# Moving the first G slice and the second X slice of a weight-gradient matmul from hardware to software DMA queues

## The chip, the cores and the metric

One core of one Trainium2 chip. The metric is the device time of the whole program in microseconds (us), as the median of several runs on one chip. The profile comes from one of those runs and counts its own span, some 1.7 us less than the device time.

The kernel before takes 176.0 us (three runs, 175.95 to 176.5).

## The reference

```python
# input 16 x 512 x 1024, grad_output 16 x 512 x 768, both float32
grad_weight = np.einsum('bmk,bmn->kn', input, grad_output)   # 1024 x 768
```

Batch and m are one contraction of 8192 rows. The kernel cuts it into 64 slices of 128 rows: X[s] is 128 x 1024, G[s] is 128 x 768. Each slice costs 12 matmuls of 512 columns, eight "wide" ones (the first 512 columns of G) and four "narrow" ones (the other 256, with G as the weights).

## The kernel before

Data is float32 in memory and bfloat16 in the matmuls. There are two ways to get it there. The loads on the *software queue* (issued by GpSimd) write bfloat16 tiles from the float32 data (its packets are counted at 1536 bytes for a row of 768). Those on the *hardware queues* (issued by sync and scalar) write float32 tiles here, which casts on the vector engine (DVE, 0.29 us for 128 x 256) or ScalarE (ACT, 0.41 us) then convert. Slice 0 and X of slice 1 come by hardware, all else by software. While data is under way, PE multiplies constants as a warm-up (0.78 to 5.42 us). Its matmuls of 512 columns start 0.427 us apart; the real ones, from the second at 5.69 us on, 0.2155 us. Below these are called half rate and full rate.

```python
ORDER = (          # A, B: wide halves; N: narrow; number: up to which slice; "!": close the sums
    "A1! B1 N1 B2! N2 A2 N3! A3 B3 A4! B5 N5 B6! N7 A6 N8! A9! B10 N9 B12! N12! A12! "
    ...
WARMUP = [512] * 10 + [128] * 2
...
    xf = [head.tile([P, K], f32, name=f"xf{s}") for s in range(2)]
    gf = head.tile([P, N], f32, name="gf")
    nc.sync.dma_start(out=gf[:, 0:NA], in_=G[0:P, 0:NA])
    nc.scalar.dma_start(out=xf[0], in_=X[0:P, :])
    nc.sync.dma_start(out=gf[:, NA:N], in_=G[0:P, NA:N])
    nc.scalar.dma_start(out=xf[1], in_=X[P : 2 * P, :])
    ...                                             # warm-up matmuls on constants
    for s in range(1, S):
        gt = xg.tile([P, N], bf16, name="gt")
        nc.gpsimd.dma_start(out=gt, in_=G[s * P : (s + 1) * P, :])
        ...
        if s > 1:
            xs[s] = xg.tile([P, K], bf16, name="xt")
            nc.gpsimd.dma_start(out=xs[s], in_=X[s * P : (s + 1) * P, :])
    ...                                             # twelve casts of g0, x0, x1
    for k in range(KS):                             # the last 14 slices, group by group
        slices = range(parts["A" if k < KS // 2 else "B"].done, S)
        pieces = [(0, NA)] if k < KS - 1 else [(0, 256), (256, 384), (384, NA)]
        for c0, c1 in pieces:
            ...                                     # matmuls of one bank
            add_out(acc[:, k, c0:c1], bank)
            W = NB if k < 6 else c1 - c0
            for c in range(c0, c1, W):
                nc.sync.dma_start(out=OUT[:, k, c : c + W], in_=acc[:, k, c : c + W])
```

Of the kernel before, what the change touches and what calls it, by code (L numbers as in the profile page):

```python
# [8 lines left out]
P = 128  # L9
NA = 512  # L10
# [6 lines left out]
ORDER = (  # L17
    "A1! B1 N1 B2! N2 A2 N3! A3 B3 A4! B5 N5 B6! N7 A6 N8! A9! B10 N9 B12! N12! A12! "
    "B15 AB17! n17! AB26! n26! AB41! n41! AB47 A50! B50! N64!"
).split()  # L20

WARMUP = [512] * 10 + [128] * 2
XBUFS = 42


# [1 line left out]
def kernel(  # L27
# [6 lines left out]
    nc = tc.nc  # L34
    bf16 = mybir.dt.bfloat16
    f32 = mybir.dt.float32

    B, M, K = input.shape
    _, _, N = grad_output.shape
    S = B * M // P  # L40
    KS = K // P
    NB = N - NA
# [3 lines left out]
    X = input.rearrange("b m k -> (b m) k")  # L46
    G = grad_output.rearrange("b m n -> (b m) n")
    OUT = out.rearrange("(ks p) n -> p ks n", p=P)

    head = ctx.enter_context(tc.tile_pool(name="head", bufs=1))  # L50
# [11 lines left out]
    xs = [None] * S  # L62
    gwide = [None] * S
    gnarrow = [None] * S
# [2 lines left out]
    ctx.enter_context(tc.manual_schedule(engines={E.PE, E.DVE, E.Activation}))  # L67


    xf = [head.tile([P, K], f32, name=f"xf{s}") for s in range(2)]  # L70
    gf = head.tile([P, N], f32, name="gf")
    nc.sync.dma_start(out=gf[:, 0:NA], in_=G[0:P, 0:NA])
    nc.scalar.dma_start(out=xf[0], in_=X[0:P, :])
    nc.sync.dma_start(out=gf[:, NA:N], in_=G[0:P, NA:N])
    nc.scalar.dma_start(out=xf[1], in_=X[P : 2 * P, :])


    ones = nc.const_aps.tensor(1.0, (P, P), bf16)
    wps = psum.tile([P, NA], f32, name="bank7")
    for i, cols in enumerate(WARMUP):  # L80
        nc.tensor.matmul(  # L81
# [5 lines left out]
        )  # L87


    for s in range(1, S):  # L90
        gt = xg.tile([P, N], bf16, name="gt")
        nc.gpsimd.dma_start(out=gt, in_=G[s * P : (s + 1) * P, :])  # L92
        gwide[s] = gt[:, 0:NA]
        gnarrow[s] = gt[:, NA:N]
        if s > 1:
            xs[s] = xg.tile([P, K], bf16, name="xt")
            nc.gpsimd.dma_start(out=xs[s], in_=X[s * P : (s + 1) * P, :])  # L97

    for s in range(2):
        xs[s] = head.tile([P, K], bf16, name=f"x{s}")  # L100
    g0 = head.tile([P, N], bf16, name="g0")
    gwide[0] = g0[:, 0:NA]
    gnarrow[0] = g0[:, NA:N]

    def round_by(engine, dst, src, c0, c1):
        copy = nc.vector.tensor_copy if engine == "DVE" else nc.scalar.copy
        copy(out=dst[:, c0:c1], in_=src[:, c0:c1])  # L107

    round_by("DVE", g0, gf, 0, 256)
    round_by("ACT", g0, gf, 256, NA)  # L110
    round_by("DVE", xs[0], xf[0], 0, P)
    round_by("ACT", xs[0], xf[0], 2 * P, 4 * P)
    round_by("DVE", xs[0], xf[0], P, 2 * P)
    round_by("DVE", xs[0], xf[0], 4 * P, 6 * P)
    round_by("ACT", xs[0], xf[0], 6 * P, 8 * P)

    def add_out(dst, src):
        nc.vector.tensor_add(out=dst, in0=src, in1=dst)  # L118

    def copy_out(dst, src, i):  # L120
        if i % 2 == 0:
            nc.vector.tensor_copy(out=dst, in_=src)  # L122
        else:
            nc.scalar.copy(out=dst, in_=src)  # L124

    def wide_mm(bank, k, s, start, stop, c0=0, c1=NA):
        nc.tensor.matmul(  # L127
            bank, xs[s][:, k * P : (k + 1) * P], gwide[s][:, c0:c1], start=start, stop=stop
        )
# [34 lines left out]
    def add_slice(part, i, s, first, last):  # L164
        group = part.groups[i]
        name, bank = part.banks[i]
        part.matmul(bank, *group, s, first, last)
        if not last:
            return
        dst = part.dst(*group)  # L170
        if part.first:
            copy_out(dst, bank, i)
            if s == 0 and i == 0:
                round_by("DVE", g0, gf, NA, N)
        else:
            add_out(dst, bank)
        if part is parts["N"] and s == S - 1:
            t, h = group
            hb = NA // SQ
            nc.vector.transpose(  # L180
                out=turned[:, h * hb : (h + 1) * hb, :, t],
                in_=dst.rearrange("p (b r) -> p b r", r=SQ),
            )
        free.append(name)
        del part.banks[i]
        if not part.banks:
            part.first = False

    def slice_by_slice(names, upto, close):
        while any(parts[n].done < upto for n in names):  # L190
            for n in names:
                part = parts[n]
                s = part.done
                if s == upto:
                    continue
                part.done += 1
                first = not part.banks
                for i in range(len(part.groups)):
                    if first:
                        open_bank(part, i)  # L200
                for i in range(len(part.groups)):
                    add_slice(part, i, s, first, close and s == upto - 1)

    def bank_by_bank(part, upto):
        first = part.done
        part.done = upto
        for i in range(len(part.groups)):
            open_bank(part, i)
            for s in range(first, upto):
                add_slice(part, i, s, s == first, s == upto - 1)  # L210

    for i, step in enumerate(ORDER):
        if i == 2:

            round_by("DVE", xs[1], xf[1], 4 * P, 6 * P)
            round_by("ACT", xs[1], xf[1], 6 * P, 8 * P)
            round_by("DVE", xs[1], xf[1], 0, 2 * P)
            round_by("ACT", xs[1], xf[1], 2 * P, 4 * P)
        close = step.endswith("!")
        names = step.rstrip("!").rstrip("0123456789")  # L220
        upto = int(step.rstrip("!").lstrip("ABNn"))
        if names.islower():
            bank_by_bank(parts[names.upper()], upto)
        else:
            slice_by_slice(names, upto, close)

    rows_of = out.rearrange("(b r) n -> r b n", r=SQ)
    for a in range(P // SQ):
        c = NA + a * NT * SQ
        nc.scalar.dma_start(  # L230
            out=rows_of[:, :, c : c + NT * SQ],
            in_=turned[a * SQ : (a + 1) * SQ].rearrange("p b r t -> p b (r t)"),
# [2 lines left out]

    for k in range(KS):
        slices = range(parts["A" if k < KS // 2 else "B"].done, S)
        pieces = [(0, NA)] if k < KS - 1 else [(0, 256), (256, 384), (384, NA)]
        for c0, c1 in pieces:
            name = free.pop(0)  # L240
            bank = psum.tile([P, NA], f32, name=name)[:, 0 : c1 - c0]
            for s in slices:
                wide_mm(bank, k, s, s == slices[0], s == slices[-1], c0, c1)
            add_out(acc[:, k, c0:c1], bank)
            free.append(name)
            W = NB if k < 6 else c1 - c0
            for c in range(c0, c1, W):
                nc.sync.dma_start(out=OUT[:, k, c : c + W], in_=acc[:, k, c : c + W])

# [29 lines left out]
```

## Time and profile before

| | before |
|---|---|
| device time, median | 176.0 us |
| span in the profile | 174.3 us |
| matrix engine (PE) busy | 169.9 us, 97% |
| 768 real matmuls at 0.2155 us | 165.5 us |
| first real matmul starts | 5.32 us |
| last add starts | 171.50 us |

Read it from both ends: since PE is the chain throughout, a change that leaves the matmuls alone can move only the start, the end, or open holes between. The prediction below shows the page, the chain, both ends and the queues.

```profile
28.78 1.03 PE L134 MATMUL bank<-xt,gt 128*128 128x512 bf16 x4
29.64 1.89 PE L127 MATMUL bank<-gt,xt 128*128 128x512 bf16 x8
31.37 1.89 PE L134 MATMUL bank<-xt,gt 128*128 128x512 bf16 x8
```

In the lines of a timeline below (start, length, engine, operation, count) gt and xt are bfloat16 tiles of G and X, gf and xf float32 ones, and out<-in stands before the sizes. The eight wide matmuls at 29.64 are slices 10 and 11 ("B12!" in the order, four each). Slice 11 is used from the fifth on, at 29.64 + 4 x 0.2155 = 30.50 us. Its X landed at 30.16 by the trace. So there is no wait, but there is only about 0.3 us to spare.

### The profile page before, as it was taken

How to read it: one execution, taken by the hardware profiler on the slowest of the kernel's cores; microseconds unless marked ns; L12 is line 12 of the kernel's file. 1: busy time of each engine (PE TensorE's matmuls, PEld its weight loads, DVE VectorE, ACT ScalarE, POOL GpSimd, SP SyncE). 2: the span in 40 equal slices, each digit the busy share in tenths (PEclk: the TensorE clock that was granted, in tenths of full speed). 3: DMA queues.
4: the chain of work that ended last, by engine and by line, in shares of the span. 5: the costliest groups of instructions: out<-in, count | busy, mean ns of one | idle time of the engine just before them, and what ended most of it. 6: DMA issues, size and time to landing. Idle time of an engine off the chain costs nothing.

```text
span 174.3 us, 2013 instructions
## 1 busy us (share of the span) xinstructions
PE 169.9 (97%) x793; PEld 78.4 (45%) x808; DVE 61.3 (35%) x103; ACT 6.2 (4%) x12; POOL 66.7 (38%) x129
## 2 busy tenths in 40 slices
PE   8999999999999999999999999999999999999993
PEld 3444444444444444444444444444444444444463
DVE  0655582883940039300000662200560003931122
ACT  2640000000000000000000000000000000000000
POOL 7444434444444444444444444444274200000000
PEclk9999999999999999999999999999999999999999
DMA  5999999999999999999999999999999990085623
GB/s 192 276 208 209 207 209 208 208 208 209 207 208 209 207 208 210 207 209 209 206 209 208 208 210 207 207 209 208 207 209 209 207 202 11 0 190 160 170 86 120
DMA packets 25048, 33.35 MB, mean 191 GB/s; under 512 B 6480, under 2 KB 16592, under 8 KB 25040
## 3 DMA queue, kind: packets, MB, share of 16 engines
q0 software_dynamic: 18000, 28.65, 89.9%
q10 hardware_dynamic: 4448, 2.10, 4.7%
q1 hardware_dynamic: 2592, 2.49, 4.2%
q8 instruction: 6, 0.10, 0.2%
q14 instruction: 2, 0.02, 0.0%
HBM read 58.72 MB, written 3.15 MB: 355 GB/s over the span
## 4 chain that ended last, share of the span: by engine, by line
PE 97%; issue 0%; DVE 0%
PE bank L127 63%; PE bank L134 32%; PE bank L81 3%; DVE acc L118 0%
## 5 line engine op out<-in xcount | busy, mean ns | idle before, releaser
L127 PE MATMUL bank<-gt,xt 128*128 128x512 bf16 (+2 forms) x515 | 108.3, 367 | 0.5
L127 PEld LDWEIGHTS <-xt 128*128 128x128 bf16 x524 | 50.2, 98 | 57.2
L118 DVE TENSOR_TENSOR acc<-bank,acc 128x512 f32<-128x512 f32 (+2 forms) x62 | 37.9, 667 | 73.4 <-PE bank L127 72.9
L134 PE MATMUL bank<-xt,gt 128*128 128x512 bf16 x242 | 54.8, 379 | 0.3
L97 POOL DMA_DIRECT2D xt<-in_input_dram x62 | 33.1, 533 | 38.7 <-DMA xt<-in_input_dram 36.5
L92 POOL DMA_DIRECT2D gt<-in_grad_output_dram x63 | 33.8, 536 | 31.2 <-DMA gt<-in_grad_output_dram 24.9
L134 PEld LDWEIGHTS <-gt 128*128 128x128 bf16 x252 | 24.6, 98 | 29.7
L118 DVE TENSOR_TENSOR acct<-bank,acct 128x512 f32<-128x512 f32 x24 | 15.7, 682 | 30.0 <-PE bank L134 29.9
L81 PE MATMUL bank<-const-bfloat16-1.0 128*128 128x512 bf16 (+1 forms) x12 | 4.6, 574 | 0.8 <-PEq L263 0.8
L81 PEld LDWEIGHTS <-const-bfloat16-1.0 128*128 128x128 bf16 x12 | 1.6, 140 | 3.5 <-issue 3.5
L122 DVE COPY acc<-bank 128x512 f32<-128x512 f32 x4 | 2.7, 687 | 1.0 <-PE bank L127 1.0
L180 DVE STREAM_TRANSPOSE turned<-acct 128x512 f32<-128x512 f32 x4 | 2.9, 715 | 0.1
L127 PEld LDWEIGHTS <-x 128*128 128x128 bf16 x16 | 1.6, 98 | 1.9 <-DVE x L107 0.2
L107 DVE CAST g<-gf 128x256 bf16<-128x256 f32 x2 | 0.6, 290 | 4.7 <-DMA gf<-in_grad_output_dram 4.7
L124 ACT COPY acc<-bank 128x512 f32<-128x512 f32 x4 | 2.1, 589 | 1.3 <-PE bank L127 1.3
L127 PE MATMUL bank<-gt,x 128*128 128x512 bf16 x8 | 2.1, 379 | 0.0
L127 PE MATMUL bank<-g,x 128*128 128x512 bf16 x8 | 2.0, 398 | 0.0
L122 DVE COPY acct<-bank 128x512 f32<-128x512 f32 x2 | 1.3, 686 | 1.3 <-PE bank L134 1.3
L107 ACT CAST x<-xf 128x256 bf16<-128x256 f32 x4 | 1.4, 409 | 0.0
L107 ACT ACT_TABLE_LOAD x1 | 1.3, 1283 | 1.7 <-PEq L263 1.7
L124 ACT COPY acct<-bank 128x512 f32<-128x512 f32 x2 | 1.1, 588 | 1.5 <-PE bank L134 1.5
L107 DVE CAST x<-xf 128x256 bf16<-128x256 f32 (+1 forms) x5 | 1.0, 260 | 0.0
(8 smaller groups left out, 3.3 us busy)
## 6 DMA issues: line engine op xcount, KB each, us to landing
xt<-in_input_dram POOLq DMA_DIRECT2D x62, 256.0 KB, 8.5
gt<-in_grad_output_dram POOLq DMA_DIRECT2D x63, 192.0 KB, 8.5
out_dram<-acc SPq DMA_DIRECT2D x13, 128.0 KB, 2.7
xf<-in_input_dram ACTq DMA_DIRECT2D x2, 512.0 KB, 5.1
out_dram<-turned ACTq DMA_DIRECT2D x4, 256.0 KB, 3.4
gf<-in_grad_output_dram SPq DMA_DIRECT2D x1, 256.0 KB, 3.9
out_dram<-acc SPq DMA_DIRECT2D x1, 256.0 KB, 2.0
gf<-in_grad_output_dram SPq DMA_DIRECT2D x1, 128.0 KB, 4.7
```

What stands on the lines that cost most here:

```text
L81: nc.tensor.matmul(wps[:, 0:cols], ones, nc.const_aps.tensor(1.0, (P, cols), bf16), start=True, stop=True,)
L92: nc.gpsimd.dma_start(out=gt, in_=G[s * P : (s + 1) * P, :])
L97: nc.gpsimd.dma_start(out=xs[s], in_=X[s * P : (s + 1) * P, :])
L107: copy(out=dst[:, c0:c1], in_=src[:, c0:c1])
L118: nc.vector.tensor_add(out=dst, in0=src, in1=dst)
L122: nc.vector.tensor_copy(out=dst, in_=src)
L124: nc.scalar.copy(out=dst, in_=src)
L127: nc.tensor.matmul(bank, xs[s][:, k * P : (k + 1) * P], gwide[s][:, c0:c1], start=start, stop=stop)
L134: nc.tensor.matmul(bank, gnarrow[s].rearrange("p (r t) -> p t r", t=NT)[:, t], xs[s][:, h * NA : (h + 1) * NA], start=start, stop=stop,)
L180: nc.vector.transpose(out=turned[:, h * hb : (h + 1) * hb, :, t], in_=dst.rearrange("p (b r) -> p b r", r=SQ),)
```

## The change

Its intent: have only X of slice 0 go through the hardware queues and the casts, half of its rows on each queue; let the software queue, whose tiles need no cast, bring all of G and the other X. The warm-up is cut a little, and the last output bank is finished in two pieces in place of three.

```diff
-WARMUP = [512] * 10 + [128] * 2
+WARMUP = [512] * 9 + [128] * 4
...
-    xf = [head.tile([P, K], f32, name=f"xf{s}") for s in range(2)]
-    gf = head.tile([P, N], f32, name="gf")
-    nc.sync.dma_start(out=gf[:, 0:NA], in_=G[0:P, 0:NA])
-    nc.scalar.dma_start(out=xf[0], in_=X[0:P, :])
-    nc.sync.dma_start(out=gf[:, NA:N], in_=G[0:P, NA:N])
-    nc.scalar.dma_start(out=xf[1], in_=X[P : 2 * P, :])
+    xf = head.tile([P, K], f32, name="xf")
+    nc.sync.dma_start(out=xf[0 : P // 2], in_=X[0 : P // 2, :])
+    nc.scalar.dma_start(out=xf[P // 2 : P], in_=X[P // 2 : P, :])
...
-    for s in range(1, S):
+    for s in range(S):
...
-        if s > 1:
+        if s > 0:
...
+    xs[0] = head.tile([P, K], bf16, name="x0")   # in place of twelve casts
+    for c in range(0, K, 512):
+        nc.vector.tensor_copy(out=xs[0][:, c : c + 256], in_=xf[:, c : c + 256])
+        nc.scalar.copy(out=xs[0][:, c + 256 : c + 512], in_=xf[:, c + 256 : c + 512])
...
-        pieces = [(0, NA)] if k < KS - 1 else [(0, 256), (256, 384), (384, NA)]
+        pieces = [(0, NA)] if k < KS - 1 else [(0, 384), (384, NA)]
...
-            W = NB if k < 6 else c1 - c0
+            W = P if k == 0 else NB if k < KS - 1 else c1 - c0
```

More of the change, by code (lines that the diff above doesn't have):

```diff
@@ L94 @@
         gnarrow[s] = gt[:, NA:N]
-        if s > 1:
+        if s > 0:
             xs[s] = xg.tile([P, K], bf16, name="xt")
             nc.gpsimd.dma_start(out=xs[s], in_=X[s * P : (s + 1) * P, :])
-    for s in range(2):
-        xs[s] = head.tile([P, K], bf16, name=f"x{s}")
-    g0 = head.tile([P, N], bf16, name="g0")
-    gwide[0] = g0[:, 0:NA]
-    gnarrow[0] = g0[:, NA:N]
-    def round_by(engine, dst, src, c0, c1):
-        copy = nc.vector.tensor_copy if engine == "DVE" else nc.scalar.copy
-        copy(out=dst[:, c0:c1], in_=src[:, c0:c1])
-    round_by("DVE", g0, gf, 0, 256)
-    round_by("ACT", g0, gf, 256, NA)
-    round_by("DVE", xs[0], xf[0], 0, P)
-    round_by("ACT", xs[0], xf[0], 2 * P, 4 * P)
-    round_by("DVE", xs[0], xf[0], P, 2 * P)
-    round_by("DVE", xs[0], xf[0], 4 * P, 6 * P)
-    round_by("ACT", xs[0], xf[0], 6 * P, 8 * P)
+    xs[0] = head.tile([P, K], bf16, name="x0")
+    for c in range(0, K, 512):
+        nc.vector.tensor_copy(out=xs[0][:, c : c + 256], in_=xf[:, c : c + 256])
+        nc.scalar.copy(out=xs[0][:, c + 256 : c + 512], in_=xf[:, c + 256 : c + 512])
     def add_out(dst, src):
@@ L172, in add_slice @@
             copy_out(dst, bank, i)
-            if s == 0 and i == 0:
-                round_by("DVE", g0, gf, NA, N)
         else:
@@ L210, in bank_by_bank @@
                 add_slice(part, i, s, s == first, s == upto - 1)
-    for i, step in enumerate(ORDER):
-        if i == 2:
-            round_by("DVE", xs[1], xf[1], 4 * P, 6 * P)
-            round_by("ACT", xs[1], xf[1], 6 * P, 8 * P)
-            round_by("DVE", xs[1], xf[1], 0, 2 * P)
-            round_by("ACT", xs[1], xf[1], 2 * P, 4 * P)
+    for step in ORDER:
         close = step.endswith("!")
```

## The prediction

> **What bounds the kernel now.** I began with the page: how busy each engine is, and the chain that ended last.
>
> ```profile
> span 174.3 us, 2013 instructions
> PE 169.9 (97%) x793; PEld 78.4 (45%) x808; DVE 61.3 (35%) x103; ACT 6.2 (4%) x12; POOL 66.7 (38%) x129
> ...
> PE 97%; issue 0%; DVE 0%
> PE bank L127 63%; PE bank L134 32%; PE bank L81 3%; DVE acc L118 0%
> ```
>
> The matrix engine is the chain from one end to the other. 3% of it is warm-up on constants (L81), the rest real matmuls. The work asks for 64 slices x (8 wide + 4 narrow) = 768 matmuls of 512 columns. In the chain of waits four of them take 0.86 us, so 0.2155 us each and 768 x 0.2155 = 165.5 us. The diff changes none of these, so it can act only on the head (before the first real matmul), on the tail (after the last), or by opening a hole in between. I therefore read the timeline at both ends. The head:
>
> ```profile
> 0.74 0.41 ACTq L73 DMA_DIRECT2D xf<-in_input_dram  x1
> 0.74 0.38 SPq L72 DMA_DIRECT2D gf<-in_grad_output_dram  x1
> ...
> 0.78 4.64 PE L81 MATMUL bank<-const-bfloat16-1.0 128*128 128x512 bf16 x12 [0.78 <-PEq L263]
> ...
> 1.23 1.20 POOL L92 DMA_DIRECT2D gt<-in_grad_output_dram  x2 [0.79 <-POOLq L263]
> ...
> 4.71 0.29 DVE L107 CAST g<-gf 128x256 bf16<-128x256 f32 x1 [4.71 <-DMA gf<-in_grad_output_dram]
> ...
> 5.04 0.56 DVE L107 CAST x<-xf 128x128 bf16<-128x128 f32 x3
> ...
> 5.32 2.04 PE L127 MATMUL bank<-g,x 128*128 128x512 bf16 x8
> ...
> 7.78 0.53 POOL L97 DMA_DIRECT2D xt<-in_input_dram  x1 [2.05 <-DMA gt<-in_grad_output_dram]
> ```
>
> Real work starts at 5.32 us, when the casts of slice 0 are ready, and the warm-up was sized to end there (0.78 + 4.64 = 5.42). From 5.32 to the last add at 171.50 is 166.2 us, 0.7 us over the matmuls' own 165.5; so there is no hole to close. The last line shows that the first G slice on the software queue had landed by 7.78 us: GpSimd, its eight completion semaphores used up, waited for it. The tail:
>
> ```profile
> 169.94 0.42 DVE L118 TENSOR_TENSOR acc<-bank,acc 128x256 f32<-128x256 f32 x1 [0.84 <-PE bank L127]
> 170.72 0.29 DVE L118 TENSOR_TENSOR acc<-bank,acc 128x128 f32<-128x128 f32 x1 [0.36 <-PE bank L127]
> 171.50 0.29 DVE L118 TENSOR_TENSOR acc<-bank,acc 128x128 f32<-128x128 f32 x1 [0.49 <-PE bank L127]
> ```
>
> After 171.50 come 0.29 us of add, the last 64 KB store (issue to landing 1.5 us) and the program's end: 174.3 - 171.5 = 2.8 us.
>
> Then the view that decides this case, the DMA queues from 1 to 5.25 us. Software descriptors were being issued from 1.23 us on, yet the software queue (q0) has no line there:
>
> ```profile
> q10 hardware_dynamic: 214, 0.81, 50.7%
> q1 hardware_dynamic: 286, 0.39, 28.8%
> ```
>
> From 5.25 to 6.5 us it has 89 packets. So its first byte moved some 4 us after its first issue, just as the smaller hardware queue (q1) ran empty. Whether that is its own start-up time or starvation by the two hardware queues, this trace can't say, and the new kernel puts the very first G on that queue.
>
> [...] warm-up weight loads come 0.42 to 0.43 us apart, twice the 0.2155 of later.
>
> **The change, part by part.**
>
> *Removed:* hardware loads of G slice 0 (384 KB) and X slice 1 (512 KB), and seven of the eleven casts. The vector engine (35% busy) and ScalarE (4%) are off the chain after 5.3 us; the casts are worth nothing by themselves.
>
> *X of slice 0:* 512 KB, half on each hardware queue. By the half-microsecond view DMA moved at 111, 201 and 250 GB/s from 1.5 to 3.0 us, which is 281 KB, then at about 410. So 524 kB are moved by 3.0 + 243/410 = 3.6 us. Landing lags: wide G and first X, 786 kB, by the same sum were moved at 4.2 and released their readers at 4.71 and 5.04, up to 0.8 later. X lands at about 4.4. The cast is now four pieces, two per engine; the first pair ends after 0.29 (DVE) and 0.41 (ACT), so the first half of X is ready at 4.8 and the rest at 5.2. X alone would let the matmuls start near 5.0.
>
> *G of slice 0* on the software queue decides. Its copy reads 393 kB; GpSimd's waits end 0.97 us apart for one G slice (7.78, 8.75) and 1.23 for one X slice, so the queue moves one G in 0.97 us. (a) If it shares from the start[...], X and G together, 917 kB, are moved at 3.0 + 636/410 = 4.55 and land at about 5.35. (b) If it starves while the hardware queues are full, it begins at about 3.6 plus a gap that I guess at 0.5, moves 0.97, lags 0.8: 5.85. (c) If 4 us from issue is its own start-up, it begins at 5.28, moves 0.97, lags 0.6 to 0.8: about 7.0.
>
> *Warm-up:* 9 x 0.427 + 4 x 0.107 = 4.27 us against 10 x 0.427 + 2 x 0.107 = 4.48, so it ends 0.21 us sooner. This gains only if data is there by 5.1. That someone sized it so finely speaks for (a).
>
> *Slices 1 and on:* X of slice 0, G0, G1, X1 are the same 1.835 MB that had landed by 7.78 before, so X1 lands at about 7.8 to 8.0 in (a) and (b). It is needed 12 matmuls (2.6 us) after the start, at 8.0 or later: no hole. After that loading takes 0.97 + 1.23 = 2.20 us a slice against 12 x 0.2155 = 2.59 of matmuls, so it stays ahead. The window of the loads from slice 42 on is unchanged.
>
> *Tail:* 384 + 128 columns in place of 256 + 128 + 128. By the difference of the adds' starts a 128-column round of 14 slices takes 0.78 us and a 256-column one 1.53, so three pieces cost 3.09 and two 3.02 + about 0.03: 0.03 us saved. The 384 store (192 KB) is issued about half a microsecond ahead of the last 64 KB and could delay it by up to 0.1. The rest of the output pieces (first group in four, seventh in two) lie 3 us or more before the end; 24 hardware DMAs in both. Tail: 0 to +0.1.
>
> *Sum.* Starts of 5.4 (a), 5.9 (b), 7.05 (c) against 5.32: +0.1, +0.6, +1.7. Against this the first real matmul took 0.37 us to the next one in the timeline, 0.15 over the warm rate; a later start pays less of that: -0.1 in (a) and (b). [...] With +0.05 for the tail: (a) +0.05, (b) +0.5, (c) +1.8 to 2.3. I give (a) half, (b) three tenths, (c) a fifth, and predict 176.2 us, just above (a).
>
> **The rivals.** *Slow software start (c):* for it, the empty q0 until 5.25; against it, the coincidence with q1 running empty, and the tuned warm-up. It would make 177.8 to 178.3. *A real gain:* if the software queue shares at once and landing is quick, the start is bounded by 917 kB at the measured rate, so not before 5.15, and then at half clock: 175.8 at best. *A hole at slice 1*, in place of the wait removed: X1 has only 0.0 to 0.3 us to spare and would leave a hole of some tenths[...]; 176.4. *Tail queueing* behind the 192 KB store: 176.1 to 176.2 alone.
>
> **Range and chances.** The run-to-run spread before is 0.3% (175.95 to 176.5). 175.6 leaves room for the best gain; 177.8 takes in the lower end of (c). Faster by 2% would be 172.5, sooner than the head can give even if real work began at 1.8 us: as good as excluded. Slower by 2% needs 179.5, G0 landing after 8.8: 2 in 100.
>
> **What would show it.** Right: the first L111 matmul between 5.3 and 5.9, released by the landing of gt rather than by a cast; q0 packets before 4.5 us; 166 us from there to the last add; 2.8 us after. Wrong: q0 silent until 5.2 again (then (c)); a wait of the matrix engine for xt at about 8; more than 2.9 us from the last add on; or the granted clock dropping after the warm-up.

The sum came to +0.05 us in (a), +0.5 in (b) and +1.8 to 2.3 in (c), on 176.0. One term of it is cut: in (c), up to +0.5 for half-rate matmuls after 2 us of idleness. So the 1.8 is 1.7 + 0.05 rounded, and the 2.3, like the rival's 178.3, has the term in it; the predicted 176.2 was set just above (a), where it plays no part. Case (a), the queues sharing from the start, was the author's assumption: in the trace of the kernel before the software queue had no packet until 5.28 us. The gap of 0.5 us in (b) and the 0.1 us for the 192 KB store are guesses. Measured later: the software queue's first packet 0.01 us after the last hardware load's first completion (3.93 and 3.92), and 0.03 us more from the last add to the end. The eight semaphores are in the trace: GpSimd issued eight loads by 5.11 us, each on a semaphore of its own, and the ninth only at 7.78, after the first had landed at 7.49.

## The result, and the profile after

The changed kernel took 176.86 us (median of four runs, 176.59 to 177.08), against 176.03 (175.95 to 176.5) of the kernel before in the same rounds. Executions over 1.5% slower than the fastest of the same kernel are left out of the means. A ratio here is the mean time of one kernel's fast runs over that of the other's fast runs of the same rounds, so not quite the ratio of the medians quoted: 1.0041, with a 95% interval of 1.0018 to 1.0063. That is within 2%, and slower by some tenths of a microsecond.

The page of the kernel after: span, busy time, and the chain that ended last.

```profile
span 175.1 us, 1997 instructions
PE 170.7 (97%) x795; PEld 77.5 (44%) x795; DVE 60.2 (34%) x97; ACT 5.2 (3%) x9; POOL 67.4 (38%) x131
...
PE bank L111 53%; PE bank L118 27%; DMA xt<-in_input_dram 15%; POOL gt L89 1%; POOL xt L94 1%; DVE acc L102 0%; POOLq L239 0%
```

PE was the whole chain before. Now 15% of it is the landing of xt, and the chain in order of time (start, length, what) shows where that ends:

```profile
21.99 9.28 DMA xt<-in_input_dram
31.27 0.05 issue
31.31 1.04 PE bank L111 x4
```

Up to 31.27 us the latest event is a transfer; only from there on is it matmuls alone. So some X slice reached PE late at 31 us. The share of 15% is no measure of loss: that loading ran beside matmuls, and what was lost is only the waits of PE. They are in the timeline, first at the head (in brackets: idle before, and what ended it).

```profile
0.73 0.55 SPq L71 DMA_DIRECT2D xf<-in_input_dram  x1
0.74 0.56 ACTq L72 DMA_DIRECT2D xf<-in_input_dram  x1
...
4.31 1.28 ACT L99 ACT_TABLE_LOAD   x1 [4.31 <-DMA xf<-in_input_dram]
5.31 0.59 DVE L98 CAST x<-xf 128x256 bf16<-128x256 f32 x2 [5.31 <-DMA xf<-in_input_dram]
...
5.80 1.89 PE L111 MATMUL bank<-gt,x 128*128 128x512 bf16 x8 [0.60 <-DMA gt<-in_grad_output_dram]
7.52 1.03 PE L118 MATMUL bank<-x,gt 128*128 128x512 bf16 x4
...
8.52 1.04 PE L111 MATMUL bank<-gt,xt 128*128 128x512 bf16 x4
```

Real work starts at 5.80, 0.48 later than before, and what released it is the landing of G's first slice at 5.76. The first cast of X was done only at 5.71, so X by itself would have held the start almost as long. The first 12 matmuls then run at full rate: eight in 7.52 - 5.80 = 1.72 us, 0.215 each. In the kernel before 12 took 5.32 to 8.06, 2.74 against 2.59 at full rate, so 0.15 us of half-rate work is no longer paid. But at 7.52 + 4 x 0.2155 = 8.38 slice 1 is due, its X landed at 8.48, and the matmul starts at 8.52: a hole of 0.14. The second hole is at slice 11:

```profile
30.12 1.03 PE L111 MATMUL bank<-gt,xt 128*128 128x512 bf16 x4
31.31 1.04 PE L111 MATMUL bank<-gt,xt 128*128 128x512 bf16 x4 [0.17 <-DMA xt<-in_input_dram]
```

Slice 11 was due at 30.12 + 4 x 0.2155 = 30.98 and came at 31.31, a hole of 0.33. (The bracket shows 0.17, because matmul ends are modelled: each such record is 0.38 us long where the next starts after 0.2155. The starts are the better measure.) X11 landed at 31.27 here and at 30.16 before: 1.1 later, while the matmuls had become only 0.48 later, and the 0.3 to spare was not enough. In the trace each load raises its semaphore 16 times, read here as one for its part on each of the 16 DMA engines, and PE went on after the last of them. Here a single one was late: the other 15 were in by 30.53, in time for 30.98, the last at 31.27. From X9 on the last engine lands 0.7 to 0.8 us after the next to last, up to X8 about 0.1; in between a 16 KB packet of the instruction queue (q8) took 0.89 us from 24.65. The kernel before has the same packet at 24.01 and the same jump at X9 (0.1 to 0.9 us). The trace doesn't name the engine, so this link is one of time; if it holds, the hole came from the late head and this packet together.

The tail, as the adds that close the last two groups:

```profile
169.23 0.69 DVE L102 TENSOR_TENSOR acc<-bank,acc 128x512 f32<-128x512 f32 x1 [2.33 <-PE bank L111]
171.50 0.56 DVE L102 TENSOR_TENSOR acc<-bank,acc 128x384 f32<-128x384 f32 x1 [1.58 <-PE bank L111]
172.28 0.29 DVE L102 TENSOR_TENSOR acc<-bank,acc 128x128 f32<-128x128 f32 x1 [0.22 <-PE bank L111]
```

From the seventh group's add to the last add it takes 3.05 us, against 3.09 before (168.41 to 171.50), and from the last add to the end 2.80 against 2.77.

| where | before | after | change, us |
|---|---|---|---|
| first real matmul | 5.32 | 5.80 | +0.48 |
| half-rate loss in the first 12 | 0.15 | 0 | -0.15 |
| hole at slice 1 | 0 | 0.14 | +0.14 |
| hole at slice 11 | 0 | 0.33 | +0.33 |
| last two groups' adds apart | 3.09 | 3.05 | -0.04 |
| last add to end | 2.77 | 2.80 | +0.03 |
| sum | | | +0.79 |

The span grew by 0.8 and the median by 0.83, so the account closes.

**Why is everything loaded a microsecond later?** The same 1.835 MB (X0, G0, G1, X1) had landed at 7.49 before and at 8.48 now, and X2, X3 and X11 are 1.0 to 1.1 late too. The DMA queues from 1 to 5.25 us (packets, MB, share of 16 engines' time), to be held against the same view in the prediction:

```profile
q0 software_dynamic: 154, 0.22, 32.3%
q10 hardware_dynamic: 80, 0.26, 25.2%
q1 hardware_dynamic: 80, 0.26, 22.9%
```

The software queue now runs before 5.25. Its packets are counted as bfloat16 (1536 bytes for a row of 768), so they stand for twice as much float32 (the page counts 58.72 MB read from memory, which is both inputs whole in float32, and 29.11 MB on this queue): the three together moved 0.26 + 0.26 + 2 x 0.22 = 0.96 MB of float32 where two queues had moved 1.20. At the software queue's steady 208 GB/s (206 to 211 in most slices of the page), 416 of float32, the missing 0.24 MB are 0.6 us of the delay by estimate. From 2 to 3 us only one hardware queue has a line:

```profile
q1 hardware_dynamic: 58, 0.23, 88.7%
```

The row halves went one after the other: q1's first packet at 2.07 and its first completion at 3.00 (the trace has 16 packets of 4 bytes at the end of each load, read here as one from each engine and called completions; the semaphore's 16 rises came later, here from 3.79 to 4.24, and the last of them is the landing); q10's first packet at 3.00, its first completion at 3.92; the software queue's first packet at 3.93. Besides, the hardware queues' first byte moved at 2.07 us and not at 1.75, after issues that took 0.55 us and not 0.4. And when the software queue had taken over, half-microsecond windows (length; busy PE, PEld, DVE, ACT, POOL; PE clock; DMA share; GB/s) show it moving less than the 208 GB/s of its steady state (both counted as bfloat16):

```profile
5.00:5.50 0.50, 0.20 (x2) 0.00 (x0) 0.19 (x1) 0.50 (x1) 0.50 (x2) 1.00 1.06 138
5.50:6.00 0.50, 0.20 (x1) 0.13 (x2) 0.41 (x2) 0.49 (x3) 0.09 (x1) 1.00 1.01 165
```

The engines count as fully busy (shares of 1.06 and 1.01), but single packets took up to 0.88 us, where the median is 0.135. What these two windows fall short of 208 GB/s is, by estimate, another 0.3 us. The casts of X run at the same time (5.31 to 6.31), but they aren't needed for such stretching: all_sw, below, has it without a cast at the head.

### The profile page after: what moved, and what is told of

Same layout as the page of the kernel before. It is cut to its first block, busy times and chain, and to the rows that moved or that the text cites. A ratio compares the mean times of both kernels' runs of the same rounds, so it can differ in the third digit from the quotient of the medians.

```text
span 175.1 us, 1997 instructions
## 1 busy us (share of the span) xinstructions
PE 170.7 (97%) x795; PEld 77.5 (44%) x795; DVE 60.2 (34%) x97; ACT 5.2 (3%) x9; POOL 67.4 (38%) x131
## 3 DMA queue, kind: packets, MB, share of 16 engines
q0 software_dynamic: 18288, 29.11, 91.1%
HBM read 58.72 MB, written 3.15 MB: 353 GB/s over the span
## 4 chain that ended last, share of the span: by engine, by line
PE 81%; DMA 15%; POOL 2%; issue 1%; DVE 0%; POOLq 0%
PE bank L111 53%; PE bank L118 27%; DMA xt<-in_input_dram 15%; POOL gt L89 1%; POOL xt L94 1%; DVE acc L102 0%; POOLq L239 0%
## 5 line engine op out<-in xcount | busy, mean ns | idle before, releaser
L111 PE MATMUL bank<-gt,xt 128*128 128x512 bf16 (+2 forms) x518 | 111.0, 373 | 0.2 <-DMA xt<-in_input_dram 0.2
L118 PE MATMUL bank<-xt,gt 128*128 128x512 bf16 x252 | 56.2, 379 | 0.0
L98 DVE CAST x<-xf 128x256 bf16<-128x256 f32 x2 | 0.6, 336 | 5.3 <-DMA xf<-in_input_dram 5.3
L111 PEld LDWEIGHTS <-x 128*128 128x128 bf16 x8 | 0.7, 97 | 1.5 <-DVE x L98 0.8
L118 PE MATMUL bank<-x,gt 128*128 128x512 bf16 x4 | 1.0, 379 | 0.0
L99 ACT CAST x<-xf 128x256 bf16<-128x256 f32 x2 | 0.7, 402 | 0.0
```

The costliest lines, as they stand in the source:

```text
L98: nc.vector.tensor_copy(out=xs[0][:, c : c + 256], in_=xf[:, c : c + 256])
L99: nc.scalar.copy(out=xs[0][:, c + 256 : c + 512], in_=xf[:, c + 256 : c + 512])
L111: nc.tensor.matmul(bank, xs[s][:, k * P : (k + 1) * P], gwide[s][:, c0:c1], start=start, stop=stop)
L118: nc.tensor.matmul(bank, gnarrow[s].rearrange("p (r t) -> p t r", t=NT)[:, t], xs[s][:, h * NA : (h + 1) * NA], start=start, stop=stop,)
```

## The experiments

All kernels gave right results. Each ratio is to the kernel before in the same rounds; that kernel's median was 175.94 to 176.18 in these. Several of these kernels have one or two runs that are 1.5 us or more longer than their others, among them the profiled ones of x_one, x_cols, g0_sw, sw_paced and sw_late: what their traces show need not hold for their usual runs.

**The theories.** S: the software queue gets its first packet only when the hardware queues' transfers run out, so what is needed first must not be on it. A: the row halves, one after the other, make everything late. Start-up: the queue needs its own 4 us from its first issue. Smaller candidates are the tail and the shorter warm-up.

### 1. X of slice 0 in one piece, or in column halves

```diff
# x_one, from after
-    nc.sync.dma_start(out=xf[0 : P // 2], in_=X[0 : P // 2, :])
-    nc.scalar.dma_start(out=xf[P // 2 : P], in_=X[P // 2 : P, :])
+    nc.sync.dma_start(out=xf, in_=X[0:P, :])
# x_cols, from after: the same two lines become
+    nc.sync.dma_start(out=xf[:, 0 : K // 2], in_=X[0:P, 0 : K // 2])
+    nc.scalar.dma_start(out=xf[:, K // 2 : K], in_=X[0:P, K // 2 : K])
```

> The changed kernel, but X of slice 0 comes as one transfer of all 128 rows on SyncE's queue. Theory A (the row halves are the cost: the second half waited for the first on the DMA engines, and the software queue waited for both, so that two half-partition transfers of 512 KB took from 2.07 to 4.5 us): the hardware queue runs empty by about 3.4 us, the software queue starts then instead of at 3.93, G0 lands at about 5.1 instead of 5.76, the first real matmul starts at about 5.15, both holes (slice 1, 0.14 us, and the one at 30.8 us, 0.33 us) shrink or vanish, and the time falls to 175.9 to 176.2. Theory B (only the bytes count): same bytes, so G0 at 5.7 again and 176.9.

> As before, but X of slice 0 in two column halves of all 128 rows, one on each hardware queue. Theory A (half of the rows is what hurts): as the single transfer, first real matmul at about 5.15 to 5.3, 175.9 to 176.3. Rival A2 (splitting over two queues is what hurts, whatever the cut): second queue again idle until the first is empty, first real matmul at 5.7 or later, 176.8.

x_one took 177.38 us (176.58 to 179.09 in its fast runs, one more at 180.47), ratio 1.0078 (1.0039 to 1.0117); x_cols 177.18 (176.66 to 178.66), ratio 1.0066 (1.0033 to 1.0099). Neither is better than the changed kernel. In x_cols the two hardware queues did run side by side, which is the same view as above, 2 to 3 us:

```profile
q1 hardware_dynamic: 90, 0.18, 55.0%
q10 hardware_dynamic: 76, 0.16, 42.4%
```

Together they moved 0.34 MB in that microsecond, as x_one's single load did, where the first row half had moved 0.23. In both kernels the hardware transfers ended sooner and the software queue began sooner, at 3.06 (x_one) and 3.22 (x_cols) against 3.93. But G0 did not land sooner: at 6.70 and 6.58 against 5.76. In x_one's profile 13 of 16 engines had delivered their part of it by 5.63 us, and the last three at 6.61 to 6.70. Its PE timeline:

```profile
6.74 2.81 PE L110 MATMUL bank<-gt,x 128*128 128x512 bf16 x8 [1.98 <-DMA gt<-in_grad_output_dram]
9.34 1.83 PE L117 MATMUL bank<-x,gt 128*128 128x512 bf16 x4
```

The profiled run (179.09 us) is one of the longer ones, and the timeline shows why it is so long: after 1.98 us of waiting four matmuls run at full rate and the next eight at half rate (all 12 take 11.01 - 6.74 = 4.27 us, not 2.59). Without these 1.68 us it would take about 177.4, where two usual runs are (177.37 and 177.39): an estimate which suggests that G0 was about as late in those; they weren't traced. x_cols's profile is a long run too (178.66). Theory A falls as the explanation of the loss: by the times, taking the serialization away brings nothing. In the profiled runs the reason is that the software queue's first transfers get stretched on a few engines. Its half about the timing stands: the row halves do delay the software queue's start.

### 2. All loads on the software queue

```diff
# all_sw, from after
-    xf = ...; nc.sync.dma_start(...); nc.scalar.dma_start(...)   # and the four casts
-        if s > 0:
+        if True:                      # X of slice 0 by GpSimd too, after G of slice 0
```

> The changed kernel with nothing on the hardware queues at the head: X of slice 0 also by the software queue, after G0, without casts. Theory S (the software queue starts only when the engine's hardware queues are empty; by itself it is quick): first software packet at about 2.6 to 3.0 us, G0 and X0 (0.97 + 1.23 us) landed at about 5.6, first real matmul at about 5.6, no hole later, 176.2 to 176.5. Rival C (its own start-up of about 2.7 us after issue, so not before 3.9): first real matmul at 6.9, 177.7.

It took 178.09 us (177.88 to 178.46), ratio 1.0115 (1.0098 to 1.0132); the profiled run, 178.22, is a usual one. With no hardware queue at work at all, the DMA queues from 2 to 3 us:

```profile
q0 software_dynamic: 38, 0.06, 38.9%
```

The first packet moved at 2.60, that is 1.36 us after the first issue at 1.24. So the queue has no start-up of 4 us; the silence before is waiting for something else. G0 landed at 4.45, but X0, the second transfer, landed from 5.41 to 7.45 on the 16 engines (14 of them by 6.61). The timeline confirms what that cost:

```profile
7.50 1.90 PE L104 MATMUL bank<-gt,xt 128*128 128x512 bf16 x8 [2.30 <-DMA xt<-in_input_dram]
```

### 3. The tail

```diff
# old_tail: after with the kernel before's pieces; new_tail: before with the new ones
-  pieces = ... [(0, 384), (384, NA)]                  # new
+  pieces = ... [(0, 256), (256, 384), (384, NA)]      # old
-  W = P if k == 0 else NB if k < KS - 1 else c1 - c0  # new (new_tail leaves out the P of k == 0)
+  W = NB if k < 6 else c1 - c0                        # old
```

> The changed kernel with the output pieces of before (last bank in three, the first group in two, the seventh in one). If the tail is worth what the trace says (from the add of the seventh group to the last add 3.05 us against 3.09): 0.04 us slower than the changed kernel, 176.9. Rival (the tail or the other output pieces carry part of the 0.8 us): 176.5 or less.

> The kernel before with the new tail alone (last bank in two pieces, every full group stored in two; 25 instead of 24 hardware transfers). If the tail is worth what the traces say (0.04 us between the add of the seventh group and the last add, nothing after it): 175.9 to 176.0, not to be told from before. Rival (the tail is worth some tenths either way): 175.7 or less, or 176.3 or more.

old_tail took 177.11 us (176.87 to 179.22), ratio 1.0075 (1.0038 to 1.0112), with one run at 179.22: too spread to say anything of 0.04 us. The other direction is quieter: new_tail took 176.02 (175.89 to 176.52), ratio 0.9995 (0.998 to 1.001). The new tail is worth nothing that can be measured. (The expectation counts 25 hardware transfers; the page has 24.)

### 4. Only one of the two moves

```diff
# x1_sw, from before: X of slice 1 by software, G0 stays on hardware
-    nc.scalar.dma_start(out=xf[1], in_=X[P : 2 * P, :])   # and its four casts
-        if s > 1:
+        if s > 0:
# g0_sw, from before: G of slice 0 by software, X0 and X1 stay on hardware
-    nc.sync.dma_start(out=gf[:, 0:NA], ...); nc.sync.dma_start(out=gf[:, NA:N], ...)   # and its three casts
-    for s in range(1, S):
+    for s in range(S):
```

> The kernel before, with only X of slice 1 moved to the software queue (its casts gone); G0 and X0 stay on the hardware queues. Theory G (of what the change moved, it is G0 on the software queue that costs; moving X1 is free because it is the same bytes in the same order): start at 5.3 as before, X1 landed by about 7.8 and needed at 8.06, no wait of the matrix engine after the start, 176.0 to 176.2. Rival L (moving any of the head's transfers to software leaves the load stream about 1 us behind, and that makes the holes): a wait for xt at about 8.1 and one at about 31 us as in the changed kernel, 176.4 to 176.6.

> The kernel before, with only G of slice 0 moved to the software queue; X0 and X1 whole on ACT's hardware queue, 1 MB. Theory S (a software packet waits until an engine's hardware ring is empty or nearly so): the software queue starts only when 1.05 MB have passed, at about 4.5, G0 lands at about 6.0 to 6.3, first real matmul then, 176.7 to 177.2. Rival (round robin, or a start-up of its own): first software packet at 2.6 to 3.9 beside the hardware queue's, G0 by 5.3 to 5.8, 176.2 to 176.6.

x1_sw took 176.35 us (176.08 to 176.86), ratio 1.0027 (1.0011 to 1.0042). Its profiled run is its best (176.08): real work started at 5.37, X1 landed at 7.98 and was used at once,

```profile
8.02 1.04 PE L126 MATMUL bank<-gt,xt 128*128 128x512 bf16 x4
```

which is 0.91 us after the last group of four began (7.11), so the hole is 0.05; there was none at slice 11. The span of this run equals that of the kernel before (174.3), so where the 0.4 us of the median lie was not traced.

g0_sw took 177.26 us (177.13 to 178.9), ratio 1.0100 (1.0066 to 1.0135). The DMA queues from 1 to 4.55 us have one line in its trace, though six loads had been issued to the software queue by then:

```profile
q10 hardware_dynamic: 253, 0.97, 74.2%
```

and PE waited for G:

```profile
6.40 3.57 PE L119 MATMUL bank<-gt,x 128*128 128x512 bf16 x8 [0.98 <-DMA gt<-in_grad_output_dram]
```

The profiled run is one of two long ones of this kernel (178.86); here too half-rate matmuls follow the wait (eight in 3.57 us). The others, 177.13 to 177.32, are 1.2 to 1.4 us over before; in the profiled run the later start is 1.08. So of the two moves, G of slice 0 is the expensive one, and X of slice 1 costs about a quarter of it. The changed kernel pays less than g0_sw; it also takes 0.5 MB off the hardware queues, and software begins at 3.93 in place of 4.59.

### 5. The warm-up

```diff
# long_warm, from after
-WARMUP = [512] * 9 + [128] * 4
+WARMUP = [512] * 10 + [128] * 6
```

> The changed kernel with warm-up until about 5.6 us (10 of 512 columns and 6 of 128) instead of 5.05, so that the 0.6 us of idleness before the first real matmul go. If the idleness costs no clock in the usual run (the trace shows 0.215 us a matmul from the first on): the same median, 176.9, but no outlier such as the 179.2 with a lower clock that one run of this head showed. Rival (the warm-up's end matters): 176.6 or less.

176.60 us (176.57 to 176.92), ratio 1.0040 (1.0028 to 1.0052), the same as the changed kernel's 1.0041. The end of the warm-up is not what is paid for.

### 6. What stretches the first software transfers?

Three kernels tried to find out, all by giving GpSimd fills to do ahead of or between the issues.

```diff
# sw_paced, from all_sw: fills between the first loads
+                nc.gpsimd.memset(pace[:, 0 : 1024 if s == 0 else 512], 0.0)
# sw_late, from all_sw: one fill of 1.80 us before the first load
+    nc.gpsimd.memset(pace, 0.0)     # 128 x 2048
# x_one_late, from x_one: one fill of 0.95 us before the first load
+    nc.gpsimd.memset(pace, 0.0)     # 128 x 1024
```

> The all-software head again, with GpSimd fill instructions between the first loads[...]. Theory D (the stretched first software transfers of x_one, x_cols and all_sw, where some engines finished X0 or G0 up to 2 us after the others, come from descriptors being written while others are fetched): the stretching goes, X0 lands at about 5.5 to 5.8 instead of 7.45, 176.1 to 176.5. Rival E (it belongs to the first software transfers, however they are issued): X0 at about 7.4 again, 178.0 or more.

> The all-software head with its first load issued about 1.9 us later (one GpSimd fill of 2048 columns ahead of it), so that software packets begin at about 4.5 instead of 2.6. Theory F (the stretching, where a few engines finish a transfer up to 2 us after the others, hangs on the time, not on the transfer: software transfers before about 5 us suffer, later ones don't): X0's engines finish within 0.7 us of each other, X0 lands at about 7.4, much as without the delay, and the time is again about 178. Theory E (it belongs to the second transfer of the queue): X0 stretched as before, landing at about 9.3, 179.9.

> X of slice 0 as one transfer, and the software queue's first load issued about 1 us later (one GpSimd fill of 1024 columns ahead of it), so that it begins at about 3.6 instead of 3.06. Theory F: less stretching of G0, landing at about 5.4 to 5.8, 176.5 to 176.8 and no outliers of 2 us. Theory E (the first software transfers are stretched whenever they run): G0 at 6.5 or later in the profile, 177.4 or more.

sw_paced: 177.89 us (177.73 to 179.42, the profiled one), ratio 1.0122 (1.0096 to 1.0148). X0 still landed from 5.37 on its first engine to 6.97 on its last, and the time is that of all_sw. The third to fifth loads were issued at 3.31, 4.29 and 5.28 in place of 2.41, 2.93 and 3.45. So theory D, by which loads issued back to back get stretched, is not borne out; how descriptors are written and fetched was supposition and is in no trace. The spread is somewhat smaller than all_sw's (1.60 against 2.04 us), in one profile each.

sw_late: 180.42 us (179.41 to 181.22, the profiled one), ratio 1.0220 (1.0182 to 1.0258), not clear against the 2% mark. Its first packet came at 3.85, 1.37 us after the issue at 2.48, which repeats the start-up of all_sw. X0 had landed on 15 engines by 7.38 and on the last at 8.04. Neither a fixed time at which the stretching ends nor a fixed place in the order fits that.

x_one_late: 176.86 us (176.59 to 177.83), ratio 1.0047 (1.0026 to 1.0069). Software began at 3.41, later than x_one's 3.06, and yet G0 landed sooner, at 4.96 to 5.80 over the engines, and PE started at 5.84:

```profile
5.84 2.26 PE L112 MATMUL bank<-gt,x 128*128 128x512 bf16 x8 [0.64 <-DMA gt<-in_grad_output_dram]
```

In time the two kernels' intervals overlap, so this is not a shown gain; it shows only that an earlier start of the software queue is not what limits. Why the first software transfers are slow on a few engines stays open. It isn't the instruction queue: between 0 and 24 us none of these traces has a packet of it.

### The first software packet against the hardware queues, over all runs

In each kernel a hardware load ends in one completion (the 4-byte packet, not the landing) on each of the 16 DMA engines. The table sets the first of these for the last hardware load beside the first packet of the software queue, in us.

| kernel | first completion of the last hardware load | first software packet |
|---|---|---|
| x_one | 3.05 | 3.06 |
| x_cols | 3.21 | 3.22 |
| x_one_late | 3.40 | 3.41 |
| long_warm | 3.87 | 3.88 |
| after | 3.92 | 3.93 |
| old_tail | 4.20 | 4.21 |
| x1_sw | 4.34 | 4.35 |
| g0_sw | 4.59 | 4.59 |
| all_sw, sw_late (no hardware load) | | 1.36, 1.37 after issue |

Eight kernels, always within 0.01 us, and g0_sw's 4.59 was expected ("at about 4.5") before it ran: theory S is shown for these. The kernel before and new_tail don't fit the simple form: their software queue starts at 5.28 in both, while their scalar queue still had its second X load on the way (completions up to 6.73 and 6.75). What ended the silence there isn't settled.

## Why the prediction was right, and where its steps failed

The total, 176.86 us, lies in the range of 175.6 to 177.8, and within 2% of before, as said. It is not at the predicted 176.2, and the steps say why.

**Matmuls untouched, so only head, tail and holes count.** Right; the account above closes to some hundredths of a microsecond with these alone.

**Which of (a), (b), (c).** Case (b) happened: software starved, G landed at 5.76 (said: 5.85) and work started at 5.80 (said: 5.9). It had only three tenths. That 5.85 came so close is luck: the queue was to begin at 4.1 (hardware done at 3.6, a gap of 0.5), move for 0.97 and lag by 0.8; it began at 3.93 with no gap, its last part closed 1.50 later, and the landing lagged by 0.33. Case (a), with half the weight, rested on the assumption that the queues share from the start, which no trace showed, and on the warm-up that looked tuned for it; experiments 1 and 4 and the table show no sharing in eight kernels, and long_warm shows that the warm-up's length says nothing. Case (c) is refuted by all_sw's 1.36 us. The failed step is this weighting: it put the prediction at 176.2, where (b) alone gave 176.5.

**X lands at about 4.4.** Failed: its first half landed at 4.24, its second at 5.29. The step divided bytes by the summed rate of two queues that had been busy side by side. Here they weren't: the row halves' first packets came one after the other (2.07 and 3.00), and the trace of the kernel before has no such pair from which this could have been read. Its cost hid behind G's: the first cast was done at 5.71 and G landed at 5.76, so X alone, said to allow a start near 5.0, would have held it to about 5.75. (In x_one_late X was cast from 4.17 on, and G, landed at 5.80, alone held the start, at 5.84.) The software queue's first packet, too, waited for these halves: the first completion of the second was at 3.92, where 3.6 was said.

**X1 lands at 7.8 to 8.0, no hole.** Failed: 8.48 and a hole of 0.14. The step was "the same 1.835 MB that had landed by 7.78 before". The bytes are the same, but the trace shows a first byte 0.3 us later, one hardware queue at work at a time, and stretched software packets at 5 to 6 us. The rival "a hole at slice 1" had it right in kind, and of the signs of being wrong this one, "a wait of the matrix engine for xt at about 8", came.

**"After that loading takes 2.20 us a slice against 2.59, so it stays ahead."** Failed, and it is the larger of the unforeseen terms: 0.33 us at slice 11. A mean over slices is no guarantee where the order isn't slice by slice. "B10 N9 B12!" runs wide matmuls ahead of the narrow ones and so uses slice 11 early, with 0.3 us to spare before the change. The load lag of 1.1 us less the matmuls' own 0.48 exceeded that. Nor does a mean show the one engine that is 0.7 us behind the others from X9 on.

**Half-rate time saved, 0.1.** Right: 0.15. **Tail, 0 to +0.1.** Right: -0.04 + 0.03, and new_tail's ratio of 0.9995 confirms it. **Range.** Terms missed in (b): +0.14 and +0.33, which is why even (b)'s 176.5 was short. **Casts.** The prediction counts eleven with seven removed; the diff has twelve and removes eight. Nothing rests on it.

No variant beat the kernel before; new_tail only equals it.

## What to carry to other kernels

What the first matmul needs should not be put on a queue that in this program began only as the other queues' loads ended (3.93 against 3.92 us); removing casts that ran beside other work gained nothing. Before saying "loading stays ahead", find the load with the least time to spare between its landing and its first use in the order of use, for a delay of all loads hits there first; and look at the last of its 16 engines, not the mean. When a load is cut into pieces, ask whether the pieces run side by side: cut by columns they did here (0.18 and 0.16 MB in the same microsecond), cut by rows they didn't (the second began at 3.00, as the first ended).

## What the traces showed of the queues and the matmul rate

- Software behind hardware: in eight kernels the software queue had no packet until the last hardware load's first completion, to 0.01 us (3.92 and 3.93 in the changed kernel); in two others it began at 5.28 with hardware packets still on the way.
- First byte: on the software queue 1.36 and 1.37 us from the start of its first issue, with no other queue at work (all_sw, sw_late). On sync's hardware queue 1.0 us (0.74 to 1.75, before) and 1.3 with row halves (0.73 to 2.07, after); on scalar's 1.3 (0.74 to 2.04, before).
- Row halves: one after the other (3.00 and 3.00). Cut by columns, two loads of 128 rows each did overlap from 2.06 us on (0.18 and 0.16 MB in the same microsecond); why the one pair does and the other doesn't, no run here shows. The row halves' issues took 0.55 us against 0.38 to 0.41.
- Matmul rate: in g0_sw's profiled run 4.6 us of warm-up, all at half rate, and a wait of 0.98 us were followed by another 3.7 us at half rate (0.427 us a matmul). In x_one's the warm-up had reached the full rate, four matmuls after a wait of 1.98 us kept it, and eight then ran at half rate; in those of the changed kernel and all_sw waits of 0.60 and 2.30 us were followed by the full rate. Which waits are safe these runs don't settle.
- The first transfers of the software queue can be stretched on a few engines: in all_sw X0 had landed on 14 engines by 6.61 us and on the last at 7.45. The traces here don't number the engines, so whether it is always the same ones isn't shown. In x_one three were late.
- ScalarE's table load (1.28 us): in the three kernels with row halves, where its first cast waits for two loads, it started only at 4.31, 4.31 and 4.47, by the profile released by a landing of xf (in the changed kernel the first half's, at 4.24), and so in the changed kernel that cast came only at 5.60; where the cast waits for one, it started at 0.74 to 1.67.
